# Hybrid encoder on one core: recurrent scores in 32x32 column tiles, and another order for the output projection

## The chip, the cores and the metric

The kernel runs on one core of one Trainium2 chip. The metric is the device time of one execution in microseconds (us); lower is better. The core has a matrix engine (TensorE; PE in the profile, its weight loads PEld), a vector engine (VectorE, DVE), an activation engine (ScalarE, ACT), a general engine (GpSimd, POOL) and a queue engine (SyncE, SP). They run side by side and wait for each other on semaphores. Matrix products write to PSUM; everything else lives in SBUF, 128 partitions wide, or in device memory.

## The reference

One encoder layer is applied to a prompt of 256 tokens and a sample of 1024 tokens (1280 together, width 1024):

```python
x = layer_norm(ALPHA * x + token_mixer(x, ...), ln1_g, ln1_b)
x = layer_norm(ALPHA * x + memory_cross_attention(x, mem, ...), ln2_g, ln2_b)
x = layer_norm(ALPHA * x + squared_relu_mlp(x, w_up, w_down), ln3_g, ln3_b)
```

The token mixer has two branches that a gate merges, and an output projection:

```python
merged = sigmoid(gate_a) * (o_a @ w_pa) + sigmoid(gate_b) * (o_b @ w_pb)
return merged @ w_out
```

`o_a` is grouped attention with rotary positions. `o_b` is the recurrent branch: four heads of width 128, run forwards and backwards over the tokens. In one direction a query at time t sees a key at time s <= t with the product of all forget gates f between them:

```python
scores[t, s] = sum_d q[t, d] * k[s, d] * exp(b[t, d] - b[s, d])   # s <= t, b = cumsum(log f)
o_intra = scores @ v
```

Across chunks of tokens a 128x128 state per head carries the rest. All inputs and outputs are fp32.

## The kernel before, in words

**Stages.** `memproj` prepares the memory's keys and values; `hgrn` (line 169) is the recurrent branch, with the gates' projections in between; `qkv` and `attention` are the attention branch; then `back(g)` (line 745) runs the merge, the output projection, the memory attention and the MLP for each of two groups of 640 tokens. Weights arrive as fp32 in 512 KB pieces into two raw buffers, and are split into a rounded high part (ACT, line 88) and a low part (DVE or POOL, line 89), since a product of full precision is made of three fp32r matmuls (lines 118 to 120, or 129 to 131).

**The scores of a head.** `scan` works on ten chunks of 128 tokens. The scores of a chunk, key by query, are built in levels. At level B (1, 2, 4, 8, 16, 32, 64) each pair of neighbouring blocks of B tokens gets its scores: queries of one block against keys of the other. Between levels the queries `qp` and keys `ks` (two planes each, one for each direction) are multiplied by the block totals of the gates (lines 267 and 269), and the totals are folded (line 271). So no exponential of a difference is needed.

Each level first gathers the keys into `ka` (line 239, ACT). Then, for each chunk and each half z of it, one fp32 matmul (line 247) makes a block of 64 keys by 64 queries: the stationary operand is 64 columns of `ka`, and the output stands in PSUM partitions 0 to 63 or 64 to 127, so that it uses one half of TensorE's columns. Below level 64 only some entries of such a block belong to the level; a mask picks them, and `copy_predicated` (line 249, DVE) merges them into `L`. The diagonal (line 224) goes into `L` first by a plain copy. A PSUM tile has 8 chunks of 64 columns, so each step takes two tiles (8 and 2 chunks). At level 64 the blocks off the diagonal go straight to the finished score matrix `A` (line 254), and `L` is copied onto its diagonal (line 258). Later `A` times the values and the state's terms give the output (line 319), which is normalised, gated and stored (lines 321 to 330). The gated tile `sg` and the next head's query `q` share one buffer.

**What sets the order.** Outside attention each engine's instruction list is ordered by the planner of the tile framework, which plays a modelled timeline through and takes, for each engine, what it expects to be ready; an engine then works its list strictly in order. So projection and gate matmuls stand between the levels' matmuls on TensorE.

**The merge and the output projection.** In `back`, `branch(db, j)` makes slice `db` of the merged activations: a projection, a product with the gate (line 775, DVE), a sum of both branches (line 777) and the split into high and low part, `mT` (lines 88 and 89). `order` is [7, 0, 1, 2, 3, 4, 5, 6], so slice 7 comes first and slice 6 last. Ahead of the last slice `w8` requests the output weights: four tiles `ws[0]` for the first 512 output columns and four `ws[1]` for the second; tile k // 2 holds slices k, and the low parts alternate between DVE and POOL. Then, for each of ten groups (token tile i, output half hf) in `NATORD1`, `mm_full` runs the eight slices in the order 0 to 7, three matmuls each, into a PSUM tile of pool `psa`; line 819 adds the residual, and after the second half of a token tile come its normalisation (`ln_tile`) and transposition (`to_T`).

Of the kernel before, what the change touches and what calls it, by code (L numbers as in the profile page):

```python
# [10 lines left out]
F32 = mybir.dt.float32  # L11
F32R = mybir.dt.float32r
F16 = mybir.dt.float16
U8 = mybir.dt.uint8
# [6 lines left out]
P = 128  # L21
# [4 lines left out]
NT = T // P  # L26
KT = D // P
# [10 lines left out]
LEVELS = [1, 2, 4, 8, 16, 32, 64]  # L38
# [4 lines left out]
BATCHES = [(0, 4), (4, 8), (8, 10)]  # L43
HBATCH = [(0, 8), (8, 10)]
H2 = P // 2
NPRE = 3
NATT = 7
HGATES = [(0, 0, (1,)), (1, 0, (0, 1)), (0, 1, (0, 1)), (1, 1, (0, 1))]
QGATES = [(0, 2, (0, 1)), (1, 2, (0, 1))]
QFIRST = 32  # L50
AGATES = [(0, 0, (0,))] + [(i % 2, NPRE + i // 2, (0,)) for i in range(2 * (NATT - NPRE))]
FILL = 16 * sum(len(x[2]) for x in AGATES)
# [3 lines left out]
XPART = [(0, 0), (0, 1), (1, 0)]  # L56
XQV = (1, 3, 5, 7)
LNC = [slice(0, 512), slice(512, 1024)]
NATORD1 = [(0, 0), (0, 1), (1, 0), (1, 1), (2, 0), (2, 1), (3, 0), (4, 0), (3, 1), (4, 1)]
NATORD = [(0, 0), (0, 1), (1, 0), (1, 1), (2, 0), (2, 1), (3, 0), (4, 0), (3, 1), (4, 1)]  # L60
W8E = (0, 1, 0, 1)
PORD = (20, 22, 42, 44)
# [7 lines left out]
class Kern:  # L70
# [98 lines left out]
    def hgrn(self, xT, hp, pj, lv, ms):  # L169
        nc, a = self.nc, self.a  # L170
        masks = self.masks
# [33 lines left out]
        def scan(h, f, ks, qp, q, v):  # L205
# [6 lines left out]
            kd = new_ka()  # L212
            A = self.t(hp, [P, NT, P], F32, "A")
# [1 line left out]
            nc.vector.tensor_tensor(qp, f, q.unsqueeze(1).broadcast_to([P, 2, T]), op=ALU.mult)  # L215

            S = self.t(hp, [P, 2, NT - 2, P], F32, "S")
            L = S.rearrange("p d c t -> p (d c t)")[:, :NT * H2].rearrange("p (c t) -> p c t", t=H2)
            for b0, b1 in HBATCH:
                ps = self.t(lv, [P, 8, H2], F32, "lv")  # L220
                for c in range(b0, b1):
                    for z in range(2):
                        x = slice(c * P + z * H2, c * P + (z + 1) * H2)
                        nc.tensor.matmul(ps[z * H2:(z + 1) * H2, c - b0], kd[:, x], q[:, x], start=True, stop=True)
                nc.scalar.copy(L[:, b0:b1], ps[:, :b1 - b0])
            F, FN = f, T
            for li, B in enumerate(LEVELS):
                nb = T // (2 * B)

                def halves(x, h0, nblk=nb, B=B):  # L230
                    if B == 1:
                        return bass.AP(tensor=x.tensor, offset=x.offset + h0 * (T + 1), ap=[x.ap[0], [2, nblk]])
                    return bass.AP(tensor=x.tensor, offset=x.offset + h0 * (T + B), ap=[x.ap[0], [2 * B, nblk], [1, B]])

                def view(x, t, n=H2, B=B):
                    return bass.AP(tensor=x.tensor, offset=x.offset + t,
                                   ap=[x.ap[0], [2 * B, n // (2 * B)], [T + B, 2], [1, B]])
                ka = new_ka()
                nc.scalar.copy(ka.rearrange("p (n h i) -> p n h i", h=2, i=B), view(ks, 0, T))
                for b0, b1 in HBATCH:  # L240
                    ps = self.t(lv, [P, 8, H2], F32, "lv")
                    for c in range(b0, b1):
                        for z in range(2):
                            x = slice(c * P + z * H2, c * P + (z + 1) * H2)

                            r = view(qp, c * P + z * H2) if B < H2 else qp[:, 1 - z, c * P + (1 - z) * H2:c * P + (2 - z) * H2]
                            nc.tensor.matmul(ps[z * H2:(z + 1) * H2, c - b0], ka[:, x], r, start=True, stop=True)  # L247
                    if B < H2:
                        nc.vector.copy_predicated(L[:, b0:b1], masks[:, li].unsqueeze(1).broadcast_to([P, b1 - b0, H2]),
                                                  ps[:, :b1 - b0])  # L250
                    else:
                        for z in range(2):
                            rows = slice(z * H2, (z + 1) * H2)
                            nc.scalar.copy(A[rows, b0:b1, (1 - z) * H2:(2 - z) * H2], ps[rows, :b1 - b0])
                if B == H2:
                    for z in range(2):
                        rows = slice(z * H2, (z + 1) * H2)
                        nc.scalar.copy(A[rows, :, z * H2:(z + 1) * H2], L[rows])

                def ftot(pl, half, F=F, FN=FN, B=B, nblk=nb):  # L260
                    x = F[:, pl, half:FN:2]
                    if B == 1:
                        return x
                    return x.unsqueeze(2).broadcast_to([P, nblk, B])
                for hf in range(2):
                    x = halves(qp, hf)
                    nc.vector.tensor_tensor(x, x, ftot(hf, 1 - hf), op=ALU.mult)
                    x = halves(ks, hf)
# [7 lines left out]
            for gi, cl, c0, n in CHUNKS:  # L276
                ps = self.t(pj, [P, 512], F32, "pj")
# [6 lines left out]
            for dr in range(2):  # L284
                order = []
# [142 lines left out]
    def attention(self, ap, psS, psT, psV, fills):  # L428
# [316 lines left out]
    def back(self, g):  # L745
        nc, a = self.nc, self.a
        t0 = g * GRP
        sp, sp1, psa, psb = self.sp, self.sp1, self.psa, self.psb
# [5 lines left out]
        mT = self.t(self.actp, [P, 2, KT, GRP], F32R, "act")  # L754
        order = list(range(NATT, KT)) + list(range(NATT))

        def sgates(db):
            sg = [self.t(sp, [P, GRP], F32, "sg", 4) for _ in range(2)]
            for j in range(2):
                if db < (NPRE if g else NATT):  # L760
                    nc.sync.dma_start(sg[j], self.g_d[j, db, :, t0:t0 + GRP])
# [35 lines left out]
        for x, db in enumerate(order):  # L797
# [9 lines left out]
            if db == order[-1]:  # L807
                ext = self.ext_slots()
                ws = self.w8("wout", ext)
# [2 lines left out]

        lg, lb = self.ln_params(1)
        x1T = self.t(self.actp, [P, 2, KT, GRP], F32R, "act")
        for i, hf in NATORD1:
            ps = self.t(psa, [P, 512], F32, "a")
            c = slice(hf * 512, hf * 512 + 512)
            self.mm_full(ps, mT, i, ws, hf)
            nc.vector.scalar_tensor_tensor(y[:, i, c], y[:, i, c], ALPHA, ps, op0=ALU.mult, op1=ALU.add)
            if hf:  # L820
                self.ln_tile(y, i, lg, lb)
                self.to_T(y, i, x1T)
# [96 lines left out]
        q = [qproj(0)]  # L919
        q.append(qproj(1))  # L920
        pr = scores(0, q.pop(0))
        for h in range(1, XH):
# [80 lines left out]
    def run(self, stop=99):  # L1003
        ctx, tc, nc, a = self.ctx, self.tc, self.nc, self.a
# [12 lines left out]
        with ExitStack() as fs:  # L1017
            pj = fs.enter_context(tc.tile_pool(name="pj", bufs=3, space=PSUM, reuse_waits="tile"))
            lv = fs.enter_context(tc.tile_pool(name="lv", bufs=3, space=PSUM, reuse_waits="tile"))
            ms = fs.enter_context(tc.tile_pool(name="ms", bufs=2, space=PSUM, reuse_waits="tile"))  # L1020
            with ExitStack() as mx:
                mp = mx.enter_context(tc.tile_pool(name="mp", bufs=6, reuse_waits="tile"))
                self.xT = [self.t(self.actp, [P, 2, KT, GRP], F32R, "act") for _ in range(2)]
                self.memproj(mp, pj)
                for g in range(2):
                    for k in range(KT):
                        self.load_act(self.xT[g], k, a["xT"][k][:, g * GRP:(g + 1) * GRP], GRP, mp)
            with ExitStack() as hs:
                hp = hs.enter_context(tc.tile_pool(name="hp", bufs=1, reuse_waits="tile"))
                self.masks = hp.tile([P, len(LEVELS) - 1, H2], U8, name="masks")  # L1030
                raw = self.t(self.rawp, [P, 1024], F32, "raw")
                nm = (len(LEVELS) - 1) * H2
                nc.gpsimd.dma_start(raw[:, :nm], a["masks"].rearrange("p l t -> p (l t)"))
                nc.vector.tensor_copy(self.masks.rearrange("p l t -> p (l t)"), raw[:, :nm])
                self.hgrn(self.xT, hp, pj, lv, ms)
# [37 lines left out]
def _layout(i):  # L1073
    f = np.float32
    A = {k: np.asarray(v) for k, v in i.items()}
    c = np.ascontiguousarray
    x = np.concatenate([A["x_prompt"][0], A["x_sample"][0]], 0)
# [11 lines left out]
    r = {"x": c(x), "xT": c(x.T.reshape(KT, P, T)), "memT": c(mem.T.reshape(KT, P, 512))}  # L1089
# [24 lines left out]
    rows = (np.arange(TS) // GW).astype(f)  # L1114
# [8 lines left out]
    r["gnorm"] = c(A["hg_gnorm"].reshape(P, 1))  # L1123
    r["ident"] = np.eye(P, dtype=f)
    ix = np.arange(P)
    r["masks"] = c(np.stack([((ix[:, None] % H2 // b) ^ (ix[None, :H2] // b)) == 1 for b in LEVELS[:-1]], 1).astype(f))
    r["wga"], r["wgb"] = tb(col["ga"]), tb(col["gb"])
    r["wpab"] = c(np.concatenate([tb(A["w_pa"][0]), tb(A["w_pb"][0])], 2))
    r["wout"] = nb(A["w_out"][0], 2, 512)
# [28 lines left out]
```

## Time and profile before

| What | us |
|---|---|
| median of 3 runs (2453.77 to 2454.65) | 2454.51 |
| the profiled execution | 2457.29 |
| its span, first to last instruction | 2455.3 |
| PE busy in it | 2384.9 (97%) |
| DVE, ACT, POOL busy | 1327.3, 860.3, 485.9 |
| scan of head 0, diagonal to the last transposition | 83.9 (169.83 to 253.75) |
| scan of head 3 | 81.5 (479.38 to 560.90) |
| mean granted TensorE clock | 0.993 |

How to read it: a matmul's busy time covers its whole way through the array, and consecutive matmuls overlap, so the step from one start to the next says what a matmul costs, not its duration. In the timeline a row has start and length in us, engine, line, operation, what is written and read, shape and count, and in brackets the idle time before it with what ended it. A row of stretches has the stretch, its length, the busy time of each engine with the number of instructions that fall in it, the granted TensorE clock, and the share and rate of the DMA engines. A row of a tile or a line has the least, middle and largest duration in ns.

### The profile page before, as it was taken

Reading aid. Unit: us, or ns where it says so; the run is one execution under the profiler, and the core shown is the slowest. Engines: PE = TensorE matmul, PEld = TensorE weight load, DVE = VectorE, ACT = ScalarE, POOL = GpSimd, SP = SyncE. Lnnn points to the kernel's source line nnn. Section 1 sums busy time; section 2 is a strip of 40 time slices with the busy share of each in tenths; the row PEclk is TensorE's granted clock in tenths of the full one; section 3 lists DMA queues with packets and bytes.
Section 4 is the critical chain, followed back from the end, with each engine's and each line's share of the span. In section 5 each row is a group of like instructions: output and inputs, shape, how many; then the busy total and the mean of one; then the engine's idle time right before and its main releaser. Section 6 shows DMA issues by size and latency. Waiting matters only on the chain.

```text
span 2455.3 us, 37301 instructions
## 1 busy us (share of the span) xinstructions
PE 2384.9 (97%) x15596; PEld 2201.5 (90%) x15596; DVE 1327.3 (54%) x2017; ACT 860.3 (35%) x1454; POOL 485.9 (20%) x420
## 2 busy tenths in 40 slices
PE   8999999999999889999999999999999999999998
PEld 7899999999887779798899999989989889999996
DVE  5135645557888866545644444476264564444435
ACT  5223323233577764224232222223223323222220
POOL 5522221216423223212100000015231210000000
PEclk9999999999999999999999999999999999999999
DMA  8711111112267667244122322235334313222211
GB/s 286 173 35 33 57 37 38 45 36 81 60 126 129 133 139 239 87 139 155 54 83 74 89 80 81 83 106 197 113 101 139 129 54 115 72 78 78 78 52 52
DMA packets 149464, 241.50 MB, mean 98 GB/s; under 512 B 81280, under 2 KB 94736, under 8 KB 148272
## 3 DMA queue, kind: packets, MB, share of 16 engines
q1 hardware_dynamic: 129408, 192.83, 27.5%
q0 software_dynamic: 19888, 46.29, 5.8%
q8 instruction: 122, 2.00, 0.3%
q14 instruction: 46, 0.38, 0.0%
HBM read 192.55 MB, written 28.05 MB: 90 GB/s over the span
## 4 chain that ended last, share of the span: by engine, by line
PE 81%; DVE 9%; DMA 4%; ACT 3%; issue 2%; POOL 0%; SPq 0%; POOLq 0%; DVEq 0%; ACTq 0%
PE a L119 9%; PE a L120 9%; PE a L118 9%; PE a L129 8%; PE a L130 8%; PE a L131 8%; PE pj L118 4%; PE pj L119 4%; PE pj L120 4%; PE lv L247 2%; PE pj L130 1%; PE pj L131 1%; PE pj L129 1%; PE of L504 1%; DVE mx L462 1%
## 5 line engine op out<-in xcount | busy, mean ns | idle before, releaser
L118 PE MATMUL a<-act,w 128*128 128x384 f32 (+1 forms) x1664 | 513.6, 309 | 1.9 <-ACT act L88 1.9
L119 PE MATMUL a<-act,w 128*128 128x384 f32 (+1 forms) x1664 | 514.5, 309 | 0.4 <-DVE act L89 0.4
L120 PE MATMUL a<-act,w 128*128 128x384 f32 (+1 forms) x1664 | 513.8, 309 | 0.0
L89 POOL TENSOR_TENSOR w<-raw,w 128x1024 fp32r<-128x1024 f32 (+2 forms) x99 | 253.6, 2564 | 541.7 <-ACT w L88 539.6
L118 PEld LDWEIGHTS a<-act,w 128*128 128x128 f32 x1664 | 315.4, 190 | 2.7 <-ACT act L88 2.2
L119 PEld LDWEIGHTS a<-act,w 128*128 128x128 f32 x1664 | 315.9, 190 | 1.2 <-DVE act L89 0.6
L120 PEld LDWEIGHTS a<-act,w 128*128 128x128 f32 x1664 | 315.6, 190 | 0.0
L88 ACT CAST w<-raw 128x1024 fp32r<-128x1024 f32 (+2 forms) x210 | 218.3, 1041 | 253.4 <-PE a L131 163.5
L118 PE MATMUL pj<-act,w 128*128 128x384 f32 (+2 forms) x688 | 221.8, 322 | 9.2 <-ACT act L88 7.7
L119 PE MATMUL pj<-act,w 128*128 128x384 f32 (+2 forms) x688 | 220.3, 320 | 0.0
L120 PE MATMUL pj<-act,w 128*128 128x384 f32 (+2 forms) x688 | 219.5, 320 | 0.0
L135 POOL TENSOR_SCALAR rs<-mv 128x1 f32<-128x1 f32 x30 | 17.3, 576 | 999.5 <-DVE mv L706 999.1
L977 DVE SCALAR_TENSOR_TENSOR y<-y,a 128x512 f32<-128x512 f32 x160 | 109.5, 685 | 165.7 <-PE a L131 165.0
L129 PE MATMUL a<-w,act 128*128 128x512 f32 x480 | 188.1, 392 | 2.4 <-ACT act L88 2.4
L130 PE MATMUL a<-w,act 128*128 128x512 f32 x480 | 188.5, 393 | 0.0
L129 PE MATMUL a<-act,act 128*128 128x512 f32 x480 | 186.8, 390 | 1.6 <-ACT act L88 1.6
L131 PE MATMUL a<-w,act 128*128 128x512 f32 x480 | 188.2, 392 | 0.0
L131 PE MATMUL a<-act,act 128*128 128x512 f32 x480 | 187.0, 390 | 0.0
L130 PE MATMUL a<-act,act 128*128 128x512 f32 x480 | 187.0, 390 | 0.0
L89 DVE TENSOR_TENSOR w<-raw,w 128x1024 fp32r<-128x1024 f32 (+1 forms) x111 | 135.5, 1221 | 64.9 <-ACT w L88 64.9
L965 DVE TENSOR_TENSOR sg<-sg 128x256 f32<-128x256 f32 (+1 forms) x128 | 62.6, 491 | 169.1 <-ACT sg L964 164.6
L88 ACT CAST act<-raw 128x1024 fp32r<-128x1024 f32 (+2 forms) x84 | 76.7, 919 | 217.8 <-PE a L131 148.2
(222 smaller groups left out, 4693.0 us busy)
## 6 DMA issues: line engine op xcount, KB each, us to landing
raw<-in_wup_dram SPq DMA_DIRECT2D x64, 512.0 KB
raw<-in_wdn_dram SPq DMA_DIRECT2D x64, 512.0 KB
raw<-in_wh_dram SPq DMA_DIRECT2D x16, 512.0 KB
raw<-in_wpab_dram SPq DMA_DIRECT2D x16, 512.0 KB
raw<-in_wout_dram SPq DMA_DIRECT2D x16, 512.0 KB
raw<-in_wxq_dram SPq DMA_DIRECT2D x16, 512.0 KB
act<-k_d POOLq DMA_DIRECT2D x8, 1024.0 KB, 6.5
act<-v_d POOLq DMA_DIRECT2D x16, 512.0 KB, 6.1
```

The source lines that it names most:

```text
L88: nc.scalar.copy(hi, src)
L89: (eng or nc.vector).tensor_tensor(lo, src, hi.bitcast(F32), op=ALU.subtract)
L118: nc.tensor.matmul(ps, wh, xh, start=st, stop=False)
L119: nc.tensor.matmul(ps, wh, xl, start=False, stop=False)
L120: nc.tensor.matmul(ps, wl, xh, start=False, stop=en)
L129: nc.tensor.matmul(ps, xh, wh, start=st, stop=False)
L130: nc.tensor.matmul(ps, xh, wl, start=False, stop=False)
L131: nc.tensor.matmul(ps, xl, wh, start=False, stop=en)
L247: nc.tensor.matmul(ps[z * H2:(z + 1) * H2, c - b0], ka[:, x], r, start=True, stop=True)
L462: nc.vector.tensor_reduce(mx[:, :len(u[2])], S, axis=AX.X, op=ALU.max, negate=True)
L965: nc.vector.tensor_tensor(r[:, :n], r[:, :n], r[:, :n], op=ALU.mult)
L977: nc.vector.scalar_tensor_tensor(y[:, i, c], y[:, i, c], ALPHA if fb == 0 else 1.0, ps, op0=ALU.mult, op1=ALU.add)
```

## The change

Two parts.

*Scores.* The diagonal and the levels 1 to 16 are now made in blocks of 32 keys by 32 queries: four matmuls a chunk, with the output in PSUM partitions 0, 32, 64 and 96 and the column tile named. All ten chunks fit one PSUM tile, so there is one copy or one `copy_predicated` a step. At level 32 the same function pairs quarter z of the keys with quarter z ^ 1 of the queries, and eight copies on ACT put these blocks and the finished `L` into `A`. Level 64 stays as it was, without the diagonal copies. The masks shrink from six of 64 columns to five of 32.

*Output projection.* The slices are taken in the order 0, 1, 2, 3, 4, 7, 5, 6: the last two to be merged come last. The groups (0,0) and (1,0) run their first seven slices before either takes its eighth, and `NATORD1` has (1,0) ahead of (0,1).

```diff
-NATORD1 = [(0, 0), (0, 1), (1, 0), (1, 1), (2, 0), (2, 1), (3, 0), (4, 0), (3, 1), (4, 1)]
+NATORD1 = [(0, 0), (1, 0), (0, 1), (1, 1), (2, 0), (2, 1), (3, 0), (4, 0), (3, 1), (4, 1)]
...
-            for b0, b1 in HBATCH:
-                ps = self.t(lv, [P, 8, H2], F32, "lv")
-                for c in range(b0, b1):
-                    for z in range(2):
-                        x = slice(c * P + z * H2, c * P + (z + 1) * H2)
-                        nc.tensor.matmul(ps[z * H2:(z + 1) * H2, c - b0], kd[:, x], q[:, x], start=True, stop=True)
-                nc.scalar.copy(L[:, b0:b1], ps[:, :b1 - b0])
+            def quarters(lhs, rhs, swap):
+                ps = self.t(lv, [P, 16, H4], F32, "lv")
+                for c in range(NT):
+                    for z in range(4):
+                        nc.tensor.matmul(ps[z * H4:(z + 1) * H4, c], lhs[:, c * P + z * H4:c * P + (z + 1) * H4],
+                                         rhs(c * P + (z ^ swap) * H4), start=True, stop=True, tile_position=(0, z * H4))
+                return ps[:, :NT]
+            nc.scalar.copy(L, quarters(kd, lambda t: q[:, t:t + H4], 0))
...
+                if B < H4:
+                    nc.vector.copy_predicated(L, masks[:, li].unsqueeze(1).broadcast_to([P, NT, H4]),
+                                              quarters(ka, lambda t: view(qp, t), 0))
+                elif B == H4:
+                    ps = quarters(ka, lambda t: qp[:, t // H4 % 2, t:t + H4], 1)
+                    for z in range(4):
+                        rows = slice(z * H4, (z + 1) * H4)
+                        nc.scalar.copy(A[rows, :, (z ^ 1) * H4:((z ^ 1) + 1) * H4], ps[rows])
+                        nc.scalar.copy(A[rows, :, z * H4:(z + 1) * H4], L[rows])
+                else:
...
-                if B == H2:
-                    for z in range(2):
-                        rows = slice(z * H2, (z + 1) * H2)
-                        nc.scalar.copy(A[rows, :, z * H2:(z + 1) * H2], L[rows])
...
+        ks = [k for k in range(KT) if k not in order[-2:]] + order[-2:]
+        pss = {}
+
+        def out(i, hf, k0, k1):
+            if k0 == 0:
+                pss[i, hf] = self.t(psa, [P, 512], F32, "a")
+            for k in ks[k0:k1]:
+                self.mm_n(pss[i, hf], mT, k, i * P, ws[hf][k // 2], (k % 2) * 512, 512, k == ks[0], k == ks[-1])
+        for x in NATORD1[:2]:
+            out(*x, 0, KT - 1)
         for i, hf in NATORD1:
-            ps = self.t(psa, [P, 512], F32, "a")
             c = slice(hf * 512, hf * 512 + 512)
-            self.mm_full(ps, mT, i, ws, hf)
+            out(i, hf, KT - 1 if (i, hf) in pss else 0, KT)
+            ps = pss[i, hf]
```

More of the change, by code (lines that the diff above doesn't have):

```diff
@@ L45 @@
 H2 = P // 2
+H4 = P // 4
 NPRE = 3
@@ L217, in scan @@
             S = self.t(hp, [P, 2, NT - 2, P], F32, "S")
-            L = S.rearrange("p d c t -> p (d c t)")[:, :NT * H2].rearrange("p (c t) -> p c t", t=H2)
-            for b0, b1 in HBATCH:
-                ps = self.t(lv, [P, 8, H2], F32, "lv")
-                for c in range(b0, b1):
-                    for z in range(2):
-                        x = slice(c * P + z * H2, c * P + (z + 1) * H2)
-                        nc.tensor.matmul(ps[z * H2:(z + 1) * H2, c - b0], kd[:, x], q[:, x], start=True, stop=True)
-                nc.scalar.copy(L[:, b0:b1], ps[:, :b1 - b0])
+            L = S.rearrange("p d c t -> p (d c t)")[:, :NT * H4].rearrange("p (c t) -> p c t", t=H4)
+            def quarters(lhs, rhs, swap):
[6 more added lines that the diff above has]
+            nc.scalar.copy(L, quarters(kd, lambda t: q[:, t:t + H4], 0))
             F, FN = f, T
@@ L233, in halves, with view @@
                     return bass.AP(tensor=x.tensor, offset=x.offset + h0 * (T + B), ap=[x.ap[0], [2 * B, nblk], [1, B]])
-                def view(x, t, n=H2, B=B):
+                def view(x, t, n=H4, B=B):
                     return bass.AP(tensor=x.tensor, offset=x.offset + t,
@@ L239, in scan @@
                 nc.scalar.copy(ka.rearrange("p (n h i) -> p n h i", h=2, i=B), view(ks, 0, T))
-                for b0, b1 in HBATCH:
-                    ps = self.t(lv, [P, 8, H2], F32, "lv")
-                    for c in range(b0, b1):
-                        for z in range(2):
[L244 to L251, printed above, removed]
+                if B < H4:
[8 more added lines that the diff above has]
+                else:
+                    for b0, b1 in HBATCH:
+                        ps = self.t(lv, [P, 8, H2], F32, "lv")
+                        for c in range(b0, b1):
+                            for z in range(2):
+                                nc.tensor.matmul(ps[z * H2:(z + 1) * H2, c - b0], ka[:, c * P + z * H2:c * P + (z + 1) * H2],
+                                                 qp[:, 1 - z, c * P + (1 - z) * H2:c * P + (2 - z) * H2], start=True, stop=True)
                         for z in range(2):
@@ L254, in scan @@
                             nc.scalar.copy(A[rows, b0:b1, (1 - z) * H2:(2 - z) * H2], ps[rows, :b1 - b0])
-                if B == H2:
-                    for z in range(2):
-                        rows = slice(z * H2, (z + 1) * H2)
-                        nc.scalar.copy(A[rows, :, z * H2:(z + 1) * H2], L[rows])
                 def ftot(pl, half, F=F, FN=FN, B=B, nblk=nb):
@@ L1029, in run @@
                 hp = hs.enter_context(tc.tile_pool(name="hp", bufs=1, reuse_waits="tile"))
-                self.masks = hp.tile([P, len(LEVELS) - 1, H2], U8, name="masks")
+                self.masks = hp.tile([P, len(LEVELS) - 2, H4], U8, name="masks")
                 raw = self.t(self.rawp, [P, 1024], F32, "raw")
-                nm = (len(LEVELS) - 1) * H2
+                nm = (len(LEVELS) - 2) * H4
                 nc.gpsimd.dma_start(raw[:, :nm], a["masks"].rearrange("p l t -> p (l t)"))
@@ L1125, in _layout @@
     ix = np.arange(P)
-    r["masks"] = c(np.stack([((ix[:, None] % H2 // b) ^ (ix[None, :H2] // b)) == 1 for b in LEVELS[:-1]], 1).astype(f))
+    r["masks"] = c(np.stack([((ix[:, None] % H4 // b) ^ (ix[None, :H4] // b)) == 1 for b in LEVELS[:-2]], 1).astype(f))
     r["wga"], r["wgb"] = tb(col["ga"]), tb(col["gb"])
```

## The prediction

> **What bounds the kernel now.** I read the page first: the engine totals and the chain that ended last.
>
> ```profile
> span 2455.3 us, 37301 instructions
> ...
> PE 2384.9 (97%) x15596; PEld 2201.5 (90%) x15596; DVE 1327.3 (54%) x2017; ACT 860.3 (35%) x1454; POOL 485.9 (20%) x420
> ...
> PE 81%; DVE 9%; DMA 4%; ACT 3%; issue 2%; POOL 0%; SPq 0%; POOLq 0%; DVEq 0%; ACTq 0%
> ```
>
> TensorE carries the chain. The question is whether that also holds where the change sits, so I cut the recurrent branch into the four heads' scans (first and last shown; columns: stretch, length, then busy time of PE, weight loads, DVE, ACT, POOL).
>
> ```profile
> 169.83:253.75 83.92, 83.92 (x839) 81.81 (x838) 51.34 (x80) 28.28 (x42) 21.47 (x16) 1.00 0.16 49
> ...
> 479.38:560.90 81.52, 81.52 (x816) 79.23 (x816) 43.20 (x73) 25.69 (x42) 19.70 (x19) 1.00 0.13 44
> ```
>
> PE has no gap at full clock: gate and projection products fill it between the levels. Here a PE microsecond saved is a microsecond of span; DVE (51 of 84) and ACT (28 of 84) have room.
>
> **What one level costs.** The timeline of PE around a level of wide blocks (first group), level 1 (second) and level 2 (third):
>
> ```profile
> 187.37 0.34 PE L118 MATMUL pj<-act,w 128*128 128x384 f32 x1
> 187.64 1.39 PE L247 MATMUL lv<-act 128*64 128x64 f32 x40
> 188.96 0.44 PE L119 MATMUL pj<-act,w 128*128 128x384 f32 x1
> ...
> 267.21 0.34 PE L119 MATMUL pj<-act,w 128*128 128x384 f32 x1
> 267.48 1.90 PE L247 MATMUL lv<-act 128*64 128x64 f32 x40
> 269.31 0.44 PE L120 MATMUL pj<-act,w 128*128 128x384 f32 x1
> ...
> 274.29 1.47 PE L247 MATMUL lv<-act 128*64 128x64 f32 x40
> ```
>
> ```profile
> L247 PE MATMUL lv<-act x1120: 221/222/288, 171.0 to 526.1; 128*64 128x64 f32 x187
> L247 PEldq EVENT_SEMAPHORE  x24: 51/51/51, 177.5 to 518.1; - x24
> ```
>
> 1120 = 4 heads x 7 levels x 20 products x 2: each fp32 product is two matmul records. Level 4 and up: 1.39 less the last one's 0.22 is 1.17 us from first to last start, 20 rounds of two column halves at 58 ns, or 29 ns a start. From neighbour to neighbour it is 1.59, less an ordinary 0.17 step 1.42, so entering and leaving the narrow shape costs 0.25. Level 1: 2.10 - 0.17 - 0.25 = 1.68 (84 ns a round; its moving operand is picked element by element from two planes). Level 2: 1.47 - 0.22 = 1.25 (62 ns).
>
> **Do column tiles overlap, and by how much?** I counted the level's matmuls begun in windows that open with the level and close ever later:
>
> ```profile
> 193.93:194.04 0.11, 0.10 (x2) 1.00 0.00 0
> 193.93:194.05 0.12, 0.11 (x4) 1.00 0.00 0
> 193.93:194.10 0.17, 0.16 (x4) 1.00 0.00 0
> 193.93:194.11 0.18, 0.17 (x6) 1.00 0.00 0
> ```
>
> The two halves start within 10 ns of each other; then nothing for 50 ns. So a start needs under 10 ns, and the round is set by the 64 columns. The full-width fp32 product gives the slope:
>
> ```profile
> 231.00 0.39 PE L319 MATMUL ms<-v,A 128*128 128x128 f32 x2
> 231.22 0.39 PE L319 MATMUL ms<-S,act 128*128 128x128 f32 x2
> ```
>
> Two in 0.22 us: 111 ns for 128 columns, 58 for 64, so 53 per 64 columns, and 58 - 26.5 = 32 ns for 32 (an estimate from these rows; four starts at 8 ns just fit). For level 1 half of 84 and half of the fixed 5: 44; level 2: 34.
>
> **The sum for the scores.** Seven calls a head become quarters (the diagonal and levels 1 to 32); the top level stays. Products double to 40, records to 80, in 20 rounds of four.
> - Before, a head: 5 x 1.17 + 1.68 + 1.25 = 8.78 us.
> - After: 20 x (5 x 32 + 44 + 34) ns = 4.76 us.
> - Saved 4.02 a head, 16.1 in all.
> - Runs of narrow matmuls: 34 now, because two heads break the diagonal in two and two break level 1. With one PSUM tile a call it is at most 32: 2 x 0.25 = 0.5.
>
> ```profile
> 259.80 1.03 PE L224 MATMUL lv<-q,act 128*64 128x64 f32 x28
> 263.36 0.57 PE L224 MATMUL lv<-q,act 128*64 128x64 f32 x12
> ```
>
> No row has a 32-column matmul, so both ends: with no fixed part 20 x 26.5 ns a call, saving some 19; at worst the instruction stream cannot supply the starts. For that end I look where the queue was nearly empty: the sequencer's event before a level came at 518.10 (last of x24 above), and its 40 starts were done 1.17 us after the first:
>
> ```profile
> 518.18 0.28 PE L118 MATMUL of<-act,w 128*128 128x256 f32 x1
> 518.39 1.39 PE L247 MATMUL lv<-act 128*64 128x64 f32 x40
> ```
>
> 518.39 + 1.17 - 518.15 = 1.41 us for 40: at most 35 ns a start. At 35 a call costs 2.8: 7 x 2.8 - 8.78 = +10.8 a head, +43. I take 32 ns a round, since the paired starts within 10 ns are the nearest row; the supply is the first rival.
>
> [...]
>
> **The other engines.** DVE merges one 128x320 tile instead of two:
>
> ```profile
> L249 DVE COPY_PREDICATED S<-masks,lv 128x512 f32<-128x512 uint8 x24 | 17.9, 744 | 87.5 <-PE lv L247 87.5
> ...
> L249 DVE COPY_PREDICATED S<-masks,lv 128x128 f32<-128x128 uint8 x24 | 7.0, 290 | 0.0
> ```
>
> 1.03 us becomes 0.52 (the line through both), and none at level 32. There ACT makes eight copies of 32x320 instead:
>
> ```profile
> L254 ACT COPY A<-lv x16: 259/420/584, 214.7 to 527.5; 64x512 f32<-64x512 f32 x8, 64x128 f32<-64x128 f32 x8
> ```
>
> About 0.42 each: 3.4 us a head, less two diagonal copies at the top. Cost nothing: ACT's 28 of 84 us hides it, and DVE's four products of the level run meanwhile; uncovered it is 4 x 3.4 = 13.6. The smaller mask load and cast come once, beside projections: nothing.
>
> **The output projection.** Here PE does stall, in the first token group:
>
> ```profile
> 993.76 0.39 PE L131 MATMUL a<-w,act 128*128 128x512 f32 x1
> 996.52 0.50 PE L129 MATMUL a<-w,act 128*128 128x512 f32 x1 [2.37 <-ACT act L88]
> 998.58 0.79 PE L129 MATMUL a<-act,act 128*128 128x512 f32 x1 [1.56 <-ACT act L88]
> 999.17 0.63 PE L129 MATMUL a<-w,act 128*128 128x512 f32 x1
> 999.60 0.63 PE L130 MATMUL a<-w,act 128*128 128x512 f32 x1
> ```
>
> ```profile
> 989.79:993.99 4.20, 4.20 (x19) 3.12 (x18) 3.90 (x7) 2.66 (x4) 0.87 (x1) 1.00 0.11 14
> ...
> 999.17:1004.95 5.78, 5.78 (x15) 4.47 (x14) 0.61 (x1) 2.09 (x2) 2.36 (x1) 0.52 0.54 150
> ```
>
> After six slices (18 matmuls at 0.23) it waits for the last merged one: 2.53 + 1.83 + 0.36 us. Then the granted clock is 0.52, and 13 steps take 0.43 instead of 0.23: 2.6. Together 7.3. The work it waits for:
>
> ```profile
> 993.12 2.57 POOL L89 TENSOR_TENSOR w<-raw,w 128x1024 fp32r<-128x1024 f32 x1 [12.45 <-ACT w L88]
> ...
> 993.40 2.58 DVE L777 TENSOR_TENSOR sg<-sg,sg 128x256 f32<-128x256 f32 x1
> ...
> 996.07 0.40 ACT L88 CAST act<-sg 128x256 fp32r<-128x256 f32 x1 [3.02 <-DVE sg L777]
> ```
>
> The new order runs seven slices of (0,0) and (1,0) first, 42 x 0.23 = 9.6 us from 989.79, to 999.4: past the slice's arrival at 996.5. But slice 7 now comes sixth, at about 993.2, and its weight tile's low half is ready only at 993.12 + 2.57 = 995.7. If the planner keeps program order, 2.3 us of stall stays, too short to count on a clock loss; if it interleaves, none. Behind such a waiting matmul stands PE's whole order, and behind that the residual sums of DVE. No DMA is added, or moved past another queue's work. I take 5.5 saved (ends 0 and 7.3). Late next is the other weight half; five groups on this half, 5 x 24 x 0.23 = 27 us, cover it. The second token group has nothing to gain:
>
> ```profile
> 1788.00:1815.00 27.00, 27.00 (x121) 22.36 (x120) 14.67 (x22) 4.91 (x5) 10.43 (x8) 1.00 0.36 117
> ```
>
> **Sum.** 16.1 + 0.5 + 5.5 = 22.1 off the profiled execution's 2457.3 (span 2455.3 and 2.0 around it): 2435.2. The median of the runs is 2.8 below that execution, so 2432.5.
>
> **Rivals.**
> 1. *The starts come too slowly* (slower). Place: seven calls a head; mechanism: the queue delivers as on average now, 29 ns a start. Price: 560 x 29 ns = 16.2 - 8.78 = +7.5 a head, +30 - 6 = +24: 2478.5. It decides from (8.78 + 6/4)/560 = 18 ns a start; halfway (24 ns) it is +13: 2467. For: no row shows more than two starts close together. Against: within a pair they do come at once, and after the empty queue nothing thinned out. [...]
> 2. *Only two quarters overlap.* 40 rounds at 32, 44, 34 ns: +0.74 a head, +3.0 - 6 = -3: 2451.5. For: only two are seen overlapping. Against: nothing in the rows ties overlap to halves.
> 3. *The cover ends at the head's end.* Between heads 0 and 1 PE already waits for the scan:
>
> ```profile
> 255.42 0.44 PE L118 MATMUL pj<-act,w 128*128 128x384 f32 x1 [1.45 <-DVE q L193]
> ```
>
> If the scan's chain does not shorten, 4.1 us at each of three handovers is lost: 2445. Against: each level's chain loses about 0.5 on PE and 0.5 on DVE.
> 4. *The tiles do not overlap at all*: 80 x 32 ns a call, +10.3 a head, +41 - 6: 2489.5. Against: the pairs above.
>
> **Chances.** The sum 0.56 (its own range 2428 to 2441: scores at 19 with 7.3, or nothing at the output and slightly longer rounds), rival 1 0.16, rival 2 0.10, rival 3 0.12, rival 4 0.03, a new stall from the planner's other order 0.03. Within 0.2% (5 us, about what this measurement can tell) falls rival 2. Faster 0.70 (the sum, rival 3, the edge of rival 1), same 0.10, slower 0.20. The range from 2427 to 2462 leaves out the upper half of rival 1 and rival 4.
>
> **What would show it.** Right: runs of 80 matmuls lasting about 0.64 us to the last start, four starts together; the merges at 0.52 us; no granted clock near 0.5 at the output. Wrong: 80 starts spread evenly over 1.5 us or more (rival 1), rounds of two (rival 2), PE idle before the next head's projection above 1.45 us (rival 3), a stall at the sixth slice.

## The result, and the profile after

The changed kernel takes 2436.74 us (median of 4 runs, 2434.54 to 2440.09) against 2454.58 (4 runs, 2453.77 to 2458.06): a ratio of 0.9921, interval 0.9909 to 0.9933. (The ratios here are taken over the timed runs and are not quotients of the medians, which would be 0.9927.) By the medians it is 17.8 us less; the sum in the prediction said 22.1. One run among those below, of e1_scores, took 3907.41 us at a mean granted clock of 0.556, where the others have 0.992 to 0.996, and is left out of its ratio. The profiled executions are 2457.29 before and 2440.09 after, 17.2 apart.

The page of the kernel after, its span, engine totals and the chain that ended last:

```profile
span 2438.0 us, 39528 instructions
...
PE 2368.4 (97%) x16716; PEld 2186.5 (90%) x16716; DVE 1320.8 (54%) x1989; ACT 867.7 (36%) x1474; POOL 483.4 (20%) x420
...
PE 82%; DVE 8%; DMA 4%; ACT 3%; issue 2%; POOL 0%; SPq 0%; POOLq 0%; DVEq 0%; ACTq 0%
```

1120 more matmuls (16716 against 15596), and PE is busy 16.5 us less. The chain is still PE's. For the changed steps, the tile `lv` (least, middle and largest duration in ns, first and last start, forms):

```profile
L225 PE MATMUL lv<-act x1920: 189/196/221, 171.7 to 503.6; 128*32 128x32 f32 x192
...
L257 PE MATMUL lv<-act x160: 222/222/270, 207.3 to 509.6; 128*64 128x64 f32 x160
...
L244 DVE COPY_PREDICATED S<-masks,lv x20: 511/526/536, 172.9 to 500.8; 128x320 f32<-128x320 uint8 x20
L250 ACT COPY A<-lv x16: 406/418/422, 203.4 to 506.5; 32x320 f32<-32x320 f32 x16
```

The merge takes 0.526 us where 0.52 was forecast, the new copies 0.418 against 0.42. (The lines have moved: 319, 718 and 819 before are 322, 721 and 833 after.) The timeline of PE around level 8, level 1 and level 64:

```profile
189.92 0.90 PE L225 MATMUL lv<-act 128*32 128x32 f32 x80
190.74 0.38 PE L120 MATMUL pj<-act,w 128*128 128x256 f32 x1
...
262.78 1.06 PE L225 MATMUL lv<-act 128*32 128x32 f32 x80
263.77 0.44 PE L120 MATMUL pj<-act,w 128*128 128x384 f32 x1
...
207.35 1.43 PE L257 MATMUL lv<-act 128*64 128x64 f32 x40
```

A call of quarters lasts 0.90 less the last one's 0.20, so 0.70 us from first to last start: 80 starts, 8.9 ns each, 35 ns a round of four. The forecast was 0.64 (32 ns). Level 1 is 1.06 - 0.20 = 0.86 (43 ns a round, forecast 44). Level 64, whose code stayed, takes 1.43 - 0.22 = 1.21 (1.17 before). How the 0.70 comes about shows in windows that open with the level at 189.92 and close ever later (here PE alone, matmuls begun in brackets, then granted clock and DMA):

```profile
189.92:190.00 0.08, 0.08 (x8) 1.00 0.00 0
189.92:190.20 0.28, 0.28 (x33) 1.00 0.00 0
189.92:190.34 0.42, 0.42 (x48) 1.00 0.00 0
189.92:190.62 0.70, 0.70 (x80) 1.00 0.00 0
```

From the 8th to the 33rd start 0.20 us, 8.0 ns each: the forecast's 32 ns a round. From the 33rd to the 80th 0.42 us, 8.9 ns each. The single starts show a bend: up to the 33rd they come in rounds of four (7, 7, 6, 12 ns apart); then, after some uneven steps, in pairs (2, then 15), 8.3 ns a start.

Cut by the same landmarks (first score product, last transposition of head 3, first matmul of the output projection, first transposition to `x1T`, last matmul), the spans compare so; e0_both is a second profiled execution of the changed kernel:

| Stretch, us | before | after | e0_both | after - before |
|---|---|---|---|---|
| ahead of the first score | 169.83 | 171.06 | 169.42 | +1.23 |
| the four scans | 390.84 | 374.39 | 374.43 | -16.45 |
| to the output projection | 429.12 | 431.75 | 431.51 | +2.63 |
| output projection to the first `to_T` | 38.98 | 34.13 | 32.46 | -4.85 |
| the rest | 1413.95 | 1414.02 | 1413.82 | +0.07 |

**The scans.** I summed PE's time on the score products from neighbour start to neighbour start, less the neighbour's ordinary step: 47.9 us before (34 runs, 1280 starts), 33.5 after (34 runs, 2400 starts), 14.4 less. PE's waits in this stretch, before and after (engine, line waited for, what, us, times, longest):

```profile
PE pj L118 <- DVE q L193: 1.5, 1, 1.5
```

```profile
PE lv L225 <- DVE act L270: 0.2, 1, 0.2
```

The wait at the hand-over from head 0 to head 1 (1.45 us, the place of rival 3) is gone. That leaves 0.6 of the 16.45 that I can't assign.

**The output projection.** The stretch from its first matmul to the first transposition, before, after and in e0_both (length, then busy time of PE, weight loads, DVE, ACT, POOL with counts, granted clock, DMA share and rate):

```profile
989.79:1028.77 38.98, 35.05 (x141) 27.94 (x141) 22.10 (x33) 8.72 (x11) 12.90 (x8) 0.91 0.31 95
```

```profile
977.20:1011.33 34.13, 32.76 (x144) 26.73 (x144) 22.02 (x33) 8.74 (x11) 11.31 (x8) 1.00 0.33 108
```

```profile
975.36:1007.82 32.46, 32.46 (x145) 26.80 (x145) 20.55 (x30) 7.54 (x9) 11.30 (x8) 1.00 0.34 114
```

The granted clock is 1.00 instead of 0.91. One wait is left in the first execution of the changed kernel and none in the second (PE busy for all of 32.46). The one, in the timeline:

```profile
984.27 0.39 PE L130 MATMUL a<-w,act 128*128 128x512 f32 x1
...
984.94 1.04 ACT L89 CAST act<-raw 128x1024 fp32r<-128x1024 f32 x1
986.03 0.73 PE L130 MATMUL a<-act,act 128*128 128x512 f32 x2 [1.37 <-ACT act L89]
```

It ends with the cast of a weight tile (984.94 + 1.04 = 985.98), not with a merged slice, and no stall stands at the sixth slice. This wait is not new. The prediction put all three waits of the profile before down to the last merged slice, but the middle one (1.56 us, ahead of 998.58) ends with such a cast too:

```profile
997.49 1.04 ACT L88 CAST act<-raw 128x1024 fp32r<-128x1024 f32 x1
```

997.49 + 1.04 is 998.53, and the matmul that then starts is an `a<-act,act`: it reads weights from a tile `act`, and `w8` puts only those of the second output half there. So 1.83 of the 7.3 us were a wait for a weight of the second half, which the planner had begun, with the 20th matmul of the stretch, before the 24 of (0,0) were done.

**What grew.** The 2.6 us between scans and output projection lie in part at the end of attention, where PE waits for the DMA that transposes `p` (the profile before first):

```profile
920.05 1.87 PE L504 MATMUL of<-act,vn 128*128 128x256 f16 x8 [4.86 <-DMA act<-p]
```

```profile
907.04 1.87 PE L507 MATMUL of<-act,vn 128*128 128x256 f16 x8 [6.17 <-DMA act<-p]
```

That is 1.3 of the 2.6 here and 0.9 in e0_both (5.75). The rest I could not pin to one place. In the one kernel below that has the scores of before (e2_output) the stretch is longer than in the profile of before too, 430.24 us, so the growth is not shown to be the change's.

### The profile page after: what moved, and what is told of

Read it like the earlier page. It is cut to its first block, busy times and chain, and to the rows that moved or that the text cites. A ratio compares the mean times of both kernels' runs of the same rounds, so it can differ in the third digit from the quotient of the medians.

```text
span 2438.0 us, 39528 instructions
## 1 busy us (share of the span) xinstructions
PE 2368.4 (97%) x16716; PEld 2186.5 (90%) x16716; DVE 1320.8 (54%) x1989; ACT 867.7 (36%) x1474; POOL 483.4 (20%) x420
## 4 chain that ended last, share of the span: by engine, by line
PE 82%; DVE 8%; DMA 4%; ACT 3%; issue 2%; POOL 0%; SPq 0%; POOLq 0%; DVEq 0%; ACTq 0%
PE a L121 9%; PE a L120 9%; PE a L119 9%; PE a L132 9%; PE a L131 9%; PE a L130 9%; PE pj L119 4%; PE pj L121 4%; PE pj L120 4%; PE pj L131 1%; PE pj L132 1%; PE pj L130 1%; PE of L507 1%; DVE act L90 1%; DVE mx L465 1%
## 5 line engine op out<-in xcount | busy, mean ns | idle before, releaser
L136 POOL TENSOR_SCALAR rs<-mv 128x1 f32<-128x1 f32 x30 | 16.6, 553 | 1000.5 <-DVE mv L709 1000.4
```

## The experiments

### Each part alone

The theory is that the parts are independent, since they lie 430 us apart. e0_both is the changed kernel again, as a yardstick on the same chip; e1_scores has its scores and the output projection of before; e2_output the reverse:

```diff
 e1_scores, against the changed kernel
-NATORD1 = [(0, 0), (1, 0), (0, 1), (1, 1), ...
+NATORD1 = [(0, 0), (0, 1), (1, 0), (1, 1), ...
-        for x in NATORD1[:2]:
-            out(*x, 0, KT - 1)
...
-            out(i, hf, KT - 1 if (i, hf) in pss else 0, KT)
+            self.mm_full(ps, mT, i, ws, hf)
 e2_output, against the changed kernel
-            nc.scalar.copy(L, quarters(kd, lambda t: q[:, t:t + H4], 0))
+            for b0, b1 in HBATCH:
...
```

> The changed kernel once more, on the chip of the next three. Theory (the two parts add, and both work on TensorE's own time): about 18 us under the kernel before, ratio 0.9915 to 0.9935. If the first measurement owed something to its chip or its moment: outside that.

> The scores as changed, the output projection as before. Theory: TensorE's time from the neighbour before to the neighbour after all narrow runs falls from 47.9 to about 33.5 us, and the wait of 1.7 us between heads 0 and 1 goes: 12 to 16 us under the kernel before, ratio about 0.994; the half-clock stretch at the output projection stays (granted clock near 0.5 for 5 to 6 us). Rival (most of the gain is the output's): 6 us or less.

> The output projection as changed, the scores as before. Theory: the 4.7 us of waits and 2.6 us of half clock of the first token group fall to one wait of 1.5 to 2 us, so 5 to 6 us under the kernel before, ratio 0.9975 to 0.998, narrow runs at 47.9 us as before. Rival (the stall only moves to the weights of the second half): 2 us or less.

Measured against one median of before (2456.44, 15 runs):

| Kernel | us | ratio | interval |
|---|---|---|---|
| e0_both | 2436.17 | 0.9920 | 0.9907 to 0.9934 |
| e1_scores | 2440.01 | 0.9938 | 0.9925 to 0.9952 |
| e2_output | 2450.55 | 0.9981 | 0.9972 to 0.9989 |

The scores are worth 16.4 us (before to e1_scores) or 14.4 (e2_output to e0_both), the output projection 5.9 or 3.8, and 0.9938 x 0.9981 = 0.9919 is the ratio of both. Both lie near what was expected (ratios of about 0.994 and of 0.9975 to 0.998). The output projection of e1_scores, which has the code of before, in the same stretch and in the timeline:

```profile
974.44:1010.08 35.64, 33.69 (x140) 27.14 (x140) 20.35 (x30) 7.33 (x9) 11.93 (x8) 0.95 0.31 103
```

```profile
978.33 0.39 PE L132 MATMUL a<-w,act 128*128 128x512 f32 x1
979.11 0.49 PE L130 MATMUL a<-w,act 128*128 128x512 f32 x1 [0.39 <-ACT act L89]
981.17 0.80 PE L130 MATMUL a<-act,act 128*128 128x512 f32 x1 [1.56 <-ACT act L89]
981.76 0.63 PE L130 MATMUL a<-w,act 128*128 128x512 f32 x1
```

The same three delays, but the first is 0.5 instead of 2.5 us, because the last merged slice is ready 4.6 us after the first matmul of the stretch instead of 6.7 (the cast that ends the wait is done at 979.06 here and at 996.47 there), and the slow steps (0.43 instead of 0.23) are seven or eight instead of 13. So the 7.3 us that I read before is one execution's; here it is some 4.2, as the timed 3.8 says.

### Do four column tiles overlap?

Two other orders of the same 80 products. e3_column goes through a column tile before it takes the next, so that neighbours are nearly always of the same tile; e4_two works on two tiles at a time:

```diff
 e3_column
-                for c in range(NT):
-                    for z in range(4):
+                for z in range(4):
+                    for c in range(NT):
 e4_two
+                for c, z in [(c, z) for h in range(2) for c in range(NT) for z in (2 * h, 2 * h + 1)]:
```

> The changed kernel with the quarters issued column tile by column tile: all ten chunks of quarter 0, then of quarter 1, and so on. The same 80 starts a call, the same result. Theory (each column tile is busy some 32 ns with a 32-column product, and only different tiles overlap): 32 ns a start, 2.5 us from first to last start instead of 0.70, 1.8 us more in each of 28 calls: about 50 us slower than the changed kernel, 2485 to 2490 us. Rival (the starts themselves set the pace, whichever tile they go to): 0.70 us a call and no change.

> The changed kernel with the quarters issued two column tiles at a time: quarters 0 and 1 of all chunks, then 2 and 3. Theory (32 ns per product in its tile, two tiles overlapping): 40 rounds of 32 ns, 16 ns a start from the first start to the last with no bend after about 32 starts, 1.27 us a call; 0.57 more in 28 calls: 16 us slower than the changed kernel, about 2453. Rival (what limits the later starts of the changed kernel is a cost per pair of tiles, not the supply): a bend after about 32 starts here too, over 1.3 us a call.

One run each, beside 2455.41 before: 2480.52 and 2448.42. Level 4 of head 0 in both timelines, e3_column first:

```profile
185.81 2.42 PE L225 MATMUL lv<-act 128*32 128x32 f32 x80
```

```profile
184.07 1.37 PE L224 MATMUL lv<-act 128*32 128x32 f32 x80
```

Less the last one's 0.20, and over 79 steps: 28 ns a start in one tile, 14.8 with two, and 8.9 with the change's four. So the tiles work side by side, all four of them, which rivals 2 and 4 denied: the fewer at a time, the longer the call. With two at a time the kernel gains 7.0 us on before, with one it loses 25.1.

The 28 is a mean that holds two things. Where the order changes from one tile to the next, the steps are short, since two tiles overlap there. Within one tile, in windows that open with the call:

```profile
185.81:185.90 0.09, 0.09 (x3) 1.00 0.00 0
185.81:186.28 0.47, 0.47 (x15) 1.00 0.13 35
```

Twelve starts in 0.38 us, 32 ns each, which is the estimate of the prediction. The short steps at the changes are most of why both runs came out under what was expected (2485 to 2490, and 2453).

Within one column tile the step from start to start is 32 ns, with 32 columns and, as e9_slow below shows, with 16; across four tiles it is 8.9 ns. So here the 32 ns belong to the tile and not to the engine.

### What sets 35 ns a round?

If a tile needs 32 and a round takes 35, something else is last. Two candidates: the columns, with some fixed part of a round, or the rate at which starts are supplied. e5_half splits each quarter into two products of 16 queries, 160 starts a call with the same number of columns:

```diff
 e5_half
                 for c in range(NT):
-                    for z in range(4):
-                        nc.tensor.matmul(ps[z * H4:(z + 1) * H4, c], ...
+                    for s in (0, 16):
+                        for z in range(4):
+                            nc.tensor.matmul(ps[z * H4:(z + 1) * H4, c, s:s + 16], ...
...
```

> The changed kernel with each quarter's 32 queries sent as two products of 16: 160 starts a call, the same result. Theory (after the first 30 or so starts, which the queue holds, instructions are supplied at one start per 8.4 ns, whatever the products need): the later starts keep 8.4 ns each, 1.3 to 1.4 us a call instead of 0.70; 0.65 more in 28 calls: 18 us slower than the changed kernel, about 2455 us. Rival (the array sets the pace: 16 columns take 32 - 13 = 19 ns a round): 40 rounds of 19 ns, 0.77 us a call, about 2 us slower than the changed kernel.

A call without a disturbance, in windows as above:

```profile
187.67:187.95 0.28, 0.28 (x33) 1.00 0.00 0
187.67:188.35 0.68, 0.68 (x80) 1.00 0.00 0
187.67:189.03 1.36, 1.36 (x160) 1.00 0.00 0
```

33 starts in 0.28 us, exactly as with 32 queries; then (1.36 - 0.28) / 127 = 8.5 ns each. The rival (19 ns a round, since there are half the columns) fell. But this alone does not show that the supply is last, because a product of 16 queries does not leave its tile any earlier. e9_slow, described below, sends the same products tile by tile; its level 4, in windows as above:

```profile
192.16:192.25 0.09, 0.09 (x3) 1.00 0.00 0
192.16:192.63 0.47, 0.47 (x15) 1.00 0.00 0
```

Again twelve starts in 0.38 us, 32 ns each. So with either width a round of four takes at least 32 ns, and only what goes beyond that asks for another cause. For the supply speak three things. The bend comes at the 33rd start with both widths. The runs with two tiles at a time, at 16 ns a start, have no such bend. And the weight load of a product, which from the third round up to the bend begins 30 ns ahead of its matmul (and nearly all along in e3_column), begins only 20 to 24 ns ahead once the pairs have set in: it comes late. So I take the supply of starts to be last from about the 33rd on, at 8.3 to 8.5 ns a start or 33 to 34 ns a round; whether that is the pace of the instructions or of the weight loads, no run separates. Why the bend comes at the 33rd start, no run shows: that a queue holds the first 30 or so, as the theory of e5_half has it, was my assumption.

But the run took 2476.42 us, 40 more than the changed kernel, and the longer calls explain only 28 x (1.36 - 0.70) = 18.5. Of the other 21, these are PE's waits in the scans:

```profile
PE lv L226 <- issue: 8.3, 7, 2.3
PE pj L120 <- issue: 2.9, 2, 1.6
PE pj L119 <- issue: 1.7, 1, 1.7
...
PE pj L121 <- issue: 0.2, 1, 0.2
```

13.1 us in 11 stops for which no engine or DMA of the program is to blame. (The other 8 I did not take apart; 2.6 of them lie in the scans, which take 408.61 us against 374.43 in e0_both.) Some of the stops stand in the middle of a run of score products:

```profile
295.81 0.75 PE L226 MATMUL lv<-act 128*32 128x16 f32 x68
298.87 0.24 PE L226 MATMUL lv<-act 128*32 128x16 f32 x5 [2.30 <-issue]
```

### What are the stops?

The DMA view of this stop (296.2 to 298.8) shows a single packet in all of it:

```profile
DMA packets 1, 0.02 MB, mean 6 GB/s; under 512 B 0, under 2 KB 0, under 8 KB 0
...
q8 instruction: 1, 0.02, 3.2%
```

It is one block of 16 KB of the instruction queue, 2.42 MB in 148 such blocks over the span; its transfer ended at 297.56, 1.3 us before PE went on. PE's starts halt 12 times for 0.36 to 2.48 us in the scans, and each time they go on 1.24 to 1.52 us after such a block has landed; with 55 blocks in the scans, one lands every 7.4 us on the mean, so this is hardly chance. So I formed the theory that the instructions themselves run out when a long run uses them too fast. PE's 37912 matmuls and weight loads make 256 for each of the 148 blocks (before: 31192 in 122 blocks, again 256), so that a block lasts 128 starts of a weight load and a matmul. Two more kernels, one run each, send the 160 products a call more slowly, and change nothing else: e9_slow column tile by column tile, e10_pairs two tiles at a time:

```diff
 e9_slow, against e5_half
-                for c in range(NT):
-                    for s in (0, 16):
-                        for z in range(4):
+                for z in range(4):
+                    for c in range(NT):
+                        for s in (0, 16):
 e10_pairs, against e5_half
+                for c, s, z in [(c, s, z) for h in range(2) for c in range(NT) for s in (0, 16) for z in (2 * h, 2 * h + 1)]:
```

> Each quarter as two products of 16 queries (160 starts a call, as many instructions as in the kernel of 16 queries before), but column tile by column tile, so that starts follow each other slowly. In the fast order PE stood still 12 times for 0.4 to 2.5 us, each time until 1.2 to 1.5 us after a transfer of the instruction queue had landed. Theory, the instructions run out: a block of 16 KB (256 instructions, 128 starts) is used up in 128 x 8.4 = 1.07 us, the longest stop was 2.48, so from request to use about 3.55 us; at a pace of 20 to 28 ns a start the block lasts 2.6 to 3.6 us, so stops within the score runs shrink to under 1.0 us (28 ns: none). Rival, the stops have another cause and come with the number of instructions: again about eight of 0.4 to 2.5 us within the scans. Scores as a whole 28 x 160 x 20 to 28 ns = 90 to 125 us against 33.5: a time of 2493 to 2530.

> The same 160 products a call, two column tiles at a time. Two tiles of 32 queries took 14.6 ns a start; with 16 queries 10 to 14.6. Theory, the instructions run out: a block of 128 starts lasts 1.3 to 1.9 us, so the longest stop is 3.55 less that, 1.7 to 2.3 us, and the stops are fewer or shorter than the 13 us that the scans held of them in the fast order. Rival: as many and as long as there (longest 2.5). The time by 28 x 160 x 10 to 14.6 ns = 45 to 65 us against 33.5, and stops of 3 to 10: 2451 to 2478.

The waits of e10_pairs, then of e9_slow, in the scans:

```profile
PE lv L224 <- issue: 5.2, 4, 1.5
```

```profile
PE lv L226 <- issue: 0.6, 1, 0.6
```

And a call of each:

```profile
187.61 2.62 PE L224 MATMUL lv<-act 128*32 128x16 f32 x160
```

```profile
192.16 4.94 PE L226 MATMUL lv<-act 128*32 128x16 f32 x160
```

| Kernel | ns a start | stops | longest gap between starts, us | 3.55 less the time of 128 starts |
|---|---|---|---|---|
| e5_half | 8.5 | 12 | 2.48 | (fitted) |
| e10_pairs | 15.3 | 4 | 1.70 | 1.59 |
| e9_slow | 29.9 | 1 | 0.80 | none |

The number of instructions is the same in all three, and the stops shrink with the pace as the theory wanted, but for one of 0.80 that it had not. All 17 end 1.24 to 1.52 us after a block has landed. The rival (stops that come with the number) fell. That the instructions run out is inferred from this; no view shows how many PE holds. The changed kernel has no stop of this kind: the 0.2 us of waits in its scans are for DVE. Its calls are 160 instructions, fewer than a block; only where the diagonal and level 1 meet, once each in two heads, are 320 in a row, and most runs of that length passed without a stop in e5_half too.

The times, 2493.87 and 2550.47, lie above my expectations, since I had compared the calls alone with a total that also holds the switches and the top level, and had taken a product of 16 queries to be cheaper than one of 32 (10 to 14.6 and 20 to 28 ns a start). Summed like the 33.5 above, the score products take 88.9 and 147.0 us. The 29.9 ns of e9_slow is again a mean with the short steps at the changes of tile in it, half as dense as in e3_column (28).

### The remaining parts of the change

e7_three carries both ideas on: level 64 too in column tiles of 32 keys (against 64 queries), and three groups of the output projection ahead. e8_plain takes the head start away and keeps the two orders:

```diff
 e7_three
-NATORD1 = [(0, 0), (1, 0), (0, 1), ...
+NATORD1 = [(0, 0), (1, 0), (2, 0), (0, 1), ...
...
-                            for z in range(2):
-                                nc.tensor.matmul(ps[z * H2:(z + 1) * H2, c - b0], ka[:, c * P + z * H2:c * P + (z + 1) * H2],
+                            for z in range(4):
+                                zq = 1 - z // 2
+                                nc.tensor.matmul(ps[z * H4:(z + 1) * H4, c - b0], ka[:, c * P + z * H4:c * P + (z + 1) * H4],
...
-        for x in NATORD1[:2]:
+        for x in NATORD1[:3]:
 e8_plain
-        for x in NATORD1[:2]:
+        for x in NATORD1[:0]:
```

> The changed kernel with two more edits: level 64 also in four column tiles (32 keys by 64 queries each), and three groups of the output projection, (0,0), (1,0), (2,0), ahead of the rest. Theory for level 64: 40 products in 10 rounds of four at 58 ns instead of 20 rounds of two, 0.58 us from first to last start instead of 1.17, with twice as many starts to 15 ns each, slower than the 8.4 ns a start that the changed kernel's later starts take: 0.5 to 0.6 us a head, 2 to 2.4 us. For the third group: the wait of 1.5 us that is left at the output projection has other work, 1 to 1.5 us. Together 3 to 4 us under the changed kernel, ratio to before about 0.991. Rival (top level limited by two tiles at a time; the planner finds another wait): within 1 us of the changed kernel.

> The changed kernel without the head start: the slices are taken in the new order and (1,0) stands ahead of (0,1), but each group runs its eight slices in one piece in program order. Theory (the seven slices of the second group are what covers the wait for slice 6): a wait of 2 to 3 us for slice 6 comes back at the first group, perhaps with a half clock after it, 3 to 6 us slower than the changed kernel. Rival (the order of the slices or the place of (1,0) does it, since the planner interleaves groups by itself): within 1 us of the changed kernel, no wait above 2 us.

e7_three: 2436.23 us, ratio to before 0.9921 (0.9907 to 0.9934), no different from e0_both. Its level 64:

```profile
205.51 1.35 PE L258 MATMUL lv<-act 128*32 128x64 f32 x80
```

1.35 less the last one's 0.22 is 1.13 us, against 1.21. My expectation was wrong in its arithmetic: the 64 queries still stream past, 57 ns a round, and two tiles of 64 keys already fill all 128 columns. The gain of the change is not that tiles are narrower. It is that two 32x32 blocks leave out the half of a 64x64 block that the step does not need, so that half the columns stream past in each of the 20 rounds (35 ns a round instead of 58); at level 64 nothing can be left out.

e8_plain: 2437.59 us (one run), within the spread of the changed kernel (2434.54 to 2440.09). Its output projection, in the same stretch:

```profile
974.54:1007.24 32.70, 32.70 (x145) 26.71 (x145) 21.07 (x31) 7.55 (x9) 11.33 (x8) 1.00 0.34 113
```

No wait and full clock without the head start: taking the late slices last and having (1,0) ahead of (0,1) is enough, because the planner interleaves the groups by itself. PE's order shows it: with the head start and without, the 33rd and 34th matmul of the stretch are already `a<-act,act`, of the second output half, which program order puts behind 48 of the first. The theory that the head start does it fell. Which of the two orders does how much, no run separates.

## Why the prediction was right, and where it was off

- **What bounds.** Right. In the scans PE has no gap, and all of the 14.4 us saved on it came through.
- **The tiles overlap.** Right: rounds of four, 7 ns from start to start within them, where the prediction had paired starts to go by. Rival 2 (2451.5) and rival 4 (2489.5) have their likeness in e4_two (2448.42) and e3_column (2480.52).
- **The round of 32 ns.** The 32 ns are what a product holds its tile, as e3_column shows, but not for the reason given: the estimate drew a line through 128 and 64 columns, and with 16 columns it is 32 as well, so the agreement at 32 columns is in part luck. The call was mis-sized: 0.70, not 0.64. The step said that four starts at 8 ns just fit. The first 33 starts take 0.28 us instead of 0.26, because the gap ahead of the second round is 33 ns instead of 12; the 47 behind the bend take 0.42 instead of 0.38. A head has six calls of 0.70 and one of 0.86: 5.06 instead of 4.76, so 4 x 0.3 = 1.2 us missing.
- **Rival 1** (the starts come too slowly) named a limit that fits the starts behind the bend, with the wrong number: 8.5 ns, not the 29 of the paired starts and not 18, its turning point. The upper bound of 35 ns a start was four times what the supply needs, because before no run of starts was dense enough to show it.
- **Runs of narrow matmuls**, 0.5 us: wrong. There are 34 as before. One PSUM tile a call did not keep the planner from breaking calls: two heads now break the diagonal into 56 and 24 starts and the top level into 4 and 36, as in these rows of head 1:

```profile
255.23 0.70 PE L225 MATMUL lv<-q,act 128*32 128x32 f32 x56
...
258.57 0.40 PE L225 MATMUL lv<-q,act 128*32 128x32 f32 x24
...
298.04 0.45 PE L257 MATMUL lv<-act 128*64 128x64 f32 x4
298.79 1.38 PE L257 MATMUL lv<-act 128*64 128x64 f32 x36
```

  With the 1.2 above that makes 1.7 of the 2.2 us by which the scores fell short (16.6 forecast, 14.4 measured); of the last 0.5, level 64 accounts for 0.2 (1.21 instead of 1.17 in each head), and the rest I did not take apart.
- **Levels 1 and 2.** 43 and 35 ns a round, forecast 44 and 34. So the elementwise operand keeps its price for level 1 (in e3_column, too, such products start 43 ns apart in their tile), and at level 2, 0.70 us like the others, it no longer shows.
- **DVE and ACT at nothing.** Right: no wait on them in the scans beyond 0.2 us.
- **Rival 3** (the cover ends at the head's end) went the other way: the 1.45 us hand-over wait vanished, a gain that the sum had left out.
- **The output projection**, 5.5 of 7.3: 4.85 in the profiles, 3.8 and 5.9 in the timed pairs. The waits for the merged slice went, and the slow steps (0.43 us, at a granted clock of 0.52) with them. But the prediction misread one term: 1.83 of the 7.3 was a wait for a weight of the second half. It took that half as covered by five groups; the planner's order reaches it with the 33rd matmul, and the wait is still there in one execution of two. The 7.3 was one execution's size, and the credit I gave the head start belongs to the orders. The stall feared at the sixth slice did not come. That its 2.3 us would be too short to count on a clock loss is not what the profile before shows: there a wait of 1.97 us (to 649.27) was followed by a granted clock of 0.50 from 649.75 to 653.10, while after one of 1.60 us (to 756.00) it was 1.00 up to 762.00.
- **Not in the sum:** 1.2 us ahead of the scans, which e0_both does not show (169.42), and 2.4 to 2.6 between scans and output, of which 0.9 to 1.3 are a longer wait for a DMA transposition. Of the profiled pair: -14.4 - 1.45 - 0.6 - 4.85 + 1.23 + 2.63 + 0.07 = -17.4. In the comparison with more runs the change is worth 20.3 (2456.44 to 2436.17), 1.8 short of the sum.

## What to carry to other kernels

When small products are spread over column tiles, cost a round as the larger of the tile's time (here 32 ns for an fp32 product of 32 columns, and no less for 16) and the number of tiles times the supply (here 8.5 ns a start). In these runs narrower tiles paid only where they left work out: the same area in four tiles instead of two (e7_three) was worth nothing (2436.23 us against 2436.17), and halving the columns again (e5_half) doubled the starts and saved no time on any of them (33 starts in 0.28 us with either width, then 8.5 ns each against 8.9). A saving read off a stall and its clock loss in one profile is worth that execution's size; another execution of the same code had little more than half of it.

## What the runs showed of the hardware

- Four column tiles took an fp32 matmul with its weight load every 8.3 ns once the starts came in pairs (the changed kernel, 80 starts a call; 8.9 with the uneven steps ahead of them) and every 8.5 ns behind the 33rd of 160 starts (e5_half); the first 33 came in rounds of 32 ns for four tiles, but for one gap of 33 ns ahead of the second round.
- An fp32 product occupied its column tile for 32 ns with 32 moving columns and for 32 with 16, each of its two records counted alone (e3_column, e9_slow).
- In runs of 320 instructions on PE, 12 stops of up to 2.48 us were met at 8.5 ns a start (e5_half), 4 of up to 1.70 at 15.3 (e10_pairs) and one of 0.80 at 29.9 (e9_slow); all ended 1.24 to 1.52 us after a 16 KB block of the instruction queue had landed. Runs of 160 instructions (the changed kernel's calls) had none.
